# A fused transformer step on one core: the last part of the down projection moved into the common sequence, and one more gate half computed by seven block products

## The chip, the cores and the metric

The kernel runs on one core of a Trainium2 chip. The engines that matter are TensorE (PE, with its weight loads PEld), VectorE (DVE), ScalarE (ACT), GpSimd (POOL) and SyncE (SP), which issues most of the loads. The metric is the device time of one execution in microseconds, as the median of several runs. The trace and the profile page come from one execution taken by the hardware profiler; its own time and its span are given below.

## The reference

One layer of a hybrid backbone over 640 tokens (128 context, 512 latent): adaptive RMSNorm, two parallel token mixers (retention and attention), a gated merge with residual, then a second adaptive RMSNorm and a gated MLP with a depthwise convolution of width 3, residual, and a final RMSNorm. The change is in the MLP alone:

```python
def conv_ffn(h, w_up, conv_w, conv_b, w_down):
    L = h.shape[1]
    u = h @ w_up                                   # 640 x 1024 times 1024 x 5632
    up = jnp.pad(u, ((0, 0), (1, 1), (0, 0)))
    uc = conv_w[0] * up[:, :L] + conv_w[1] * up[:, 1:L + 1] + conv_w[2] * up[:, 2:L + 2] + conv_b
    a, g = jnp.split(uc, 2, axis=-1)               # value half, gate half: 2816 columns each
    return (jax.nn.silu(g) * a) @ w_down           # 2816 x 1024
...
xs = xs + g2 * conv_ffn(h, w_up[l], conv_w[l], conv_b[l], w_down[l])
...
y_sample = rmsnorm(xs, final_g)
```

All inputs are float32. The kernel splits each operand into a high part of the type fp32r and a remainder, and a product is three matmuls: high x high, high x remainder, remainder x high.

## The kernel before

**Tiling.** The 2816 columns of the MLP are 22 blocks of 128, called `f`; two neighbours form a pair `p` (0 to 10). For each pair there is a value half (`i` = 0) and a gate half (`i` = 1). The normalised input, with columns for the convolution's edges, is `h2`: two tiles (high and remainder) of 8 blocks of rows by 2 x 322 columns. Up products are made in column pieces of 322 (`HW`), one PSUM bank each.

**Two forms of an up half.** `plain_group(p, i)` (line 1259) computes it directly: four pieces (two blocks, two column halves) of 8 x 3 = 24 matmuls, 96 in all, with `up_cols` (line 1119). `unit_group(p, i)` (line 1283) uses a scheme of seven block products (numbered m = 1, 5, 6, 2, 3, 7, 4 in their order): each is 4 x 3 = 12 matmuls of 322 columns, 84 in all, on sums and differences of quarters. The sums of weight blocks are formed for every half by VectorE in the raw weight buffer, and the sums of quarters of `h2` once, in `sa[1]` to `sa[4]`. `sa[4]` is made last, by `last_sum` (line 1203), and overwrites the quarter `aq[1, 0]` of `h2` itself. Product m3 reads `sa[4]`; m2, m3, m6, m7 and m4 add onto results of earlier ones, m6, m7 and m4 in m1's bank. Before, pair 0 and both halves of pair 1 are computed directly, and pairs 2 to 10 by block products.

**After the up products.** ScalarE and VectorE copy the banks into `ub`; `conv(f, i)` (line 1130) makes a row of 641 from it (four such row buffers, tag `row`), and `gate(f)` (line 1139) computes the activation of block `f` and writes it, high part and remainder, into the tiles `gt0` and `gt1`, one pair of tiles per pair of blocks, two buffers each. These functions are put on a list `later`, of which one is issued behind each TensorE item.

**Down products.** `down_groups` (line 1356) multiplies finished blocks with rows of `w_down` (blocks 0 and 1, then four blocks at a time), for 5 row tiles `t` and two halves of 512 output columns, into banks `acc`; partial sums are collected in `x1`. The last four blocks, 18 to 21, are treated apart behind the loop: `last_mm` runs first halves (parts 0 and 1, that is blocks 18 and 19) for four row tiles and both column halves, which fill all eight banks, and then the second halves (blocks 20 and 21); each finished bank is scaled and added by `down_add`, squared, and `finish` normalises and writes out.

**Weights.** `w_raw` loads 1 MB into one of two raw buffers (tag `raw`) through SP's queue. `w_split` (line 138) makes high parts by a ScalarE cast (line 146), and remainders in one of two ways: by VectorE's subtraction (line 151), or, with `"dma"`, by a negated ScalarE pass (line 148) and an accumulating DMA of GpSimd (line 149). The results live in eight tiles (tag `wh`) of 1024 columns. A block product takes one such tile, half of a down group of four blocks takes four.

**The order around the change.** The groups form one list; TensorE's items are issued in that order by hand (`manual_schedule`), except that the seventh product of a `unit_group` (m4) is held back until two items of the next group have gone. The weight preparations are sorted by the place of their first product, and `pump` (line 1404) issues a load when fewer than two loaded groups still have preparations open, and a preparation when it and the live ones fit into eight tiles. The order on ScalarE, VectorE and the queues within these limits is fixed at compile time. The last w_down part was outside: its two halves were loaded and split behind the loop, with VectorE's subtraction, and its first products followed the last m4.

Of the kernel before, what the change touches and what calls it, by code (L numbers as in the profile page):

```python
# [18 lines left out]
P = 128  # L19
DM = 1024  # L20
KD = DM // P
NT = 5
# [4 lines left out]
NF = FF // P  # L27
# [41 lines left out]
def hybrid_step(ctx: ExitStack, tc: tile.TileContext, a: dict, o: dict):  # L69
# [60 lines left out]
    def load_w(src, kk, n, lo_eng=None):  # L130
        return w_split(w_raw(src, kk, n), kk, n, lo_eng)

    def w_raw(src, kk, n):
        raw = wp([P, 4 * 512], F32, tag="raw", bufs=2)
        nc.sync.dma_start(raw[:, :kk * n].rearrange("p (k n) -> p k n", n=n), src.rearrange("(k p) n -> p k n", p=P))
        return raw

    def w_split(raw, kk, n, lo_eng=None):
        hs, ls = [], []
        step = 1024 // n  # L140
        for k0 in range(0, kk, step):
            w = min(step, kk - k0) * n
            rv = raw[:, k0 * n:k0 * n + w]
            hi = wp([P, 1024], F32R, tag="wh", bufs=8)[:, :w]
            lo = wp([P, 1024], F32R, tag="wh", bufs=8)[:, :w]
            nc.scalar.copy(hi, rv)  # L146
            if lo_eng == "dma":
                nc.scalar.activation(lo, rv, AF.Copy, scale=-1.0)
                nc.gpsimd.dma_start(lo, rv, accum_op=ALU.add)
            else:  # L150
                (lo_eng or V).tensor_sub(lo, rv, hi.bitcast(F32))  # L151
            for k in range(w // n):
                hs.append(hi[:, k * n:(k + 1) * n])
                ls.append(lo[:, k * n:(k + 1) * n])
        return hs, ls

    def mm3(ps, ah, al, bh, bl, start, stop):
        nc.tensor.matmul(ps, ah, bh, start=start, stop=False)  # L158
        nc.tensor.matmul(ps, ah, bl, start=False, stop=False)  # L159
        nc.tensor.matmul(ps, al, bh, start=False, stop=stop)  # L160
# [127 lines left out]
    mm = Pool("mm1", 5, space=PSUM)  # L288
# [233 lines left out]
    for i in (1, 0):  # L522
        ct, st = ctab[i], stab[i]
# [72 lines left out]
    mm = Pool("mm2", 1, space=PSUM)  # L596
# [129 lines left out]
    mm = Pool("mm3", 5, space=PSUM)  # L726
# [118 lines left out]
    st = states()  # L845
# [168 lines left out]
    def gt_pair():  # L1014
        return [gtp([P, 2, 2 * HW], F32R, tag=f"gt{i}", bufs=2) for i in range(2)]
# [7 lines left out]
    def x_row(dtype=F32):  # L1023
        return x1p([P, 768], dtype, tag="row", bufs=4)
# [3 lines left out]
    w_out, w_up, w_down = a["w_out"][0], a["w_up"][0], a["w_down"][0]  # L1028
# [40 lines left out]
    raw = w_raw(w_up[:, :256], 8, 256)  # L1069
# [6 lines left out]
    with tc.manual_schedule(engines={ET.PE}):  # L1076
        bank = {}
# [52 lines left out]
    def conv(f, i):  # L1130
        u, q = ub[f % 2][i], i * NF + f
        v = cvs[f, i] = x_row()[:, :641]
        nc.scalar.activation(v, u[:, 1:642], AF.Identity, scale=cw[:, 1, q:q + 1], bias=cw[:, 3, q:q + 1])
        V.scalar_tensor_tensor(v, u[:, 0:641], cw[:, 0, q:q + 1], v, op0=ALU.mult, op1=ALU.add)
        V.scalar_tensor_tensor(v, u[:, 2:643], cw[:, 2, q:q + 1], v, op0=ALU.mult, op1=ALU.add)
# [3 lines left out]
    def gate(f):  # L1139
        if f // 2 not in gts:  # L1140
            gts[f // 2] = gt_pair()
        r = [x[:, f % 2, :641] for x in gts[f // 2]]
        ca, cg = cvs[f, 0], cvs[f, 1]
        tg = t7([P, 641], tag="tg", bufs=1)
        nc.scalar.activation(tg, cg, AF.Tanh, scale=0.5)
        V.scalar_tensor_tensor(cg, tg, 1.0, cg, op0=ALU.add, op1=ALU.mult)
        V.tensor_mul(ca, ca, cg)
        nc.scalar.copy(r[0], ca)
        V.tensor_sub(r[1], ca, r[0].bitcast(F32))
# [17 lines left out]
    acc = Pool("acc7", 4, space=PSUM)  # L1167
    mm = Pool("mm7", 4, space=PSUM)
# [88 lines left out]
    later = []  # L1257

    def plain_group(p, i):
        st = {}  # L1260

        def load():
            st["raw"] = w_raw(w_up[:, i * FF + 2 * p * P:i * FF + 2 * (p + 1) * P], 8, 256)

        def prep():
            st["w"] = w_split(st["raw"], 8, 256, "dma")

        def bank(f, h):
            def go():
                up_cols(f, i, st["w"], h * HW, (h + 1) * HW)  # L1270
                if h:
                    if i and f % 2:
                        last_sum()
                    later.append(lambda: conv(f, i))
                    if i and f % 2:
                        later.append(lambda: gate(f - 1))
                        later.append(lambda: gate(f))
            return go

        items = [bank(2 * p + f, h) for f in range(2) for h in range(2)]  # L1280
        return load, [(prep, 4, items)], items
# [74 lines left out]
    def down_groups(fs, step, after=()):  # L1356
        rows = slice(fs[0] * P, (fs[-1] + 1) * P)

        def group(g):
            st = {}  # L1360

            def load():
                st["raw"] = w_raw(w_down[rows, g * 512:(g + 1) * 512], len(fs), 512)

            def prep():
                st["w"] = w_split(st["raw"], len(fs), 512, "dma")

# [12 lines left out]

    d0 = down_groups([0, 1], 0)
    groups = [plain_group(1, 0), d0[0], plain_group(1, 1), d0[1]]
    for p in range(2, NF // 2):
        groups += [unit_group(p, 0), unit_group(p, 1)]
        if p % 2:
            d = down_groups(list(range(2 * p - 4, 2 * p)), 2 if p == 9 else 1, (2 * p + 1, 2 * p))
            groups = groups[:-1] + [d[0], groups[-1], d[1]]
    seq, held = [], []
    for _, _, items in groups:
        for x in items[:-1] if len(items) == 7 else items:  # L1390
# [34 lines left out]
    for fn in later:  # L1425
        fn()

    fs = list(range(NF - 4, NF))
    rows = slice(fs[0] * P, NF * P)
    ws = [load_w(w_down[rows, g * 512:(g + 1) * 512], 4, 512) for g in range(2)]  # L1430
    fg = wp([P, 4 * 512], F32, tag="raw", bufs=2)[:, :DM]
    nc.sync.dma_start(fg, a["final_g"].unsqueeze(0).to_broadcast([P, DM]))
    cols = {t: ((0, 512), (512, 256), (768, 256)) if t == NT - 1 else ((0, 512), (512, 512)) for t in range(NT)}
    bank = {}

    def last_mm(t, c0, n, part):
        if (t, c0) not in bank:
            pool, tag = ((acc, "acc"), (mm, "mm"))[t % 2]
            bank[t, c0] = pool([P, 512], tag=tag)[:, :n]
        g, cc = c0 // 512, slice(c0 % 512, c0 % 512 + n)  # L1440
        down_mm(bank[t, c0], t, fs, [[x[:, cc] for x in y] for y in ws[g]], part)

    with tc.manual_schedule(engines={ET.DVE, ET.PE}):
        for t in range(NT - 1):
            for c0, n in cols[t]:
                last_mm(t, c0, n, (0, 1))
        for t in range(NT):
            for c0, n in cols[t]:
                last_mm(t, c0, n, (2, 3) if t < NT - 1 else (0, 1, 2, 3))
                down_add(bank[t, c0], t, c0)  # L1450
                square(t, c0, n)
                if c0 == 0 and t == 3:
                    finish(0, 3)
        finish(NT - 2, 2)
# [37 lines left out]
```

## Time and profile before

| | us |
|---|---|
| median of 3 runs | 1202.6 (1199.58 to 1203.64) |
| profiled execution, its time | 1202.29 |
| its span, first to last instruction | 1200.5 |
| TensorE busy | 1160.6 |
| VectorE busy | 736.5 |
| ScalarE busy | 567.1 |
| mean granted TensorE clock | 0.992 |
| gate half of pair 1, on TensorE | 790.86 to 805.16 |
| last block product and first halves of the last down products | 1151.40 to 1168.27 |
| second halves, to the last matmul | 1168.27 to 1185.3 |

How to read it: times inside the span count from its start. A busy share is a mean over stages with different limits. A row of an instruction gives its start, its length, engine and line, what it writes and reads, and in brackets the idle time of its engine before it and what ended it. Tiles have a name and a running number, such as `weights.wh.396`.

### The profile page before, as it was taken

The page shows a single profiled execution, that of the slowest core. Times are in us where ns is not written, and L with a number is a line of the kernel's source. Part 1 is how long each engine was busy: PE and PEld are TensorE (multiplying, and loading weights), DVE is VectorE, ACT ScalarE, POOL GpSimd, SP SyncE. Part 2 cuts the span into 40 slices and gives each one's busy share as a digit, 9 for nine tenths or more (in the row PEclk, how much of TensorE's full clock was granted, in tenths as well). Part 3 has the DMA queues.
Part 4 walks back from the last instruction along what each step waited for, and adds up shares of the span by engine and source line. Part 5 has one row for each costly group of instructions (what it writes and reads, how often), then busy time and mean ns, then how long its engine had stood idle before and what let it go on. Part 6 is the DMA issues. An engine that isn't in the chain of part 4 may idle for free.

```text
span 1200.5 us, 18330 instructions
## 1 busy us (share of the span) xinstructions
PE 1160.6 (97%) x7329; PEld 1043.8 (87%) x7329; DVE 736.5 (61%) x1428; ACT 567.1 (47%) x1013; POOL 173.9 (14%) x181
## 2 busy tenths in 40 slices
PE   4999999999999999999999999999999999999994
PEld 3788899999988888889999988999899898998884
DVE  5676977763234436453323259947677597677877
ACT  4345756551132324433322236667557465574453
POOL 0032200000012100042111122011111121122102
PEclk9999999999999999999999999999999999999998
DMA  8832111115564431112122459346657556677532
GB/s 283 273 113 71 36 36 36 36 59 166 198 215 148 141 97 44 36 36 70 39 92 82 158 126 184 89 113 116 139 140 170 131 105 133 128 136 171 120 96 87
DMA packets 129509, 139.54 MB, mean 116 GB/s; under 512 B 26240, under 2 KB 96976, under 8 KB 129424
## 3 DMA queue, kind: packets, MB, share of 16 engines
q1 hardware_dynamic: 104432, 109.01, 28.1%
q0 software_dynamic: 24272, 28.05, 14.4%
q8 instruction: 57, 0.93, 0.3%
q10 hardware_dynamic: 720, 1.31, 0.3%
q14 instruction: 28, 0.23, 0.1%
HBM read 110.31 MB, written 6.03 MB: 97 GB/s over the span
## 4 chain that ended last, share of the span: by engine, by line
PE 82%; DVE 8%; ACT 3%; issue 2%; DMA 2%; POOL 1%; SPq 0%; DVEq 0%; ACTq 0%; POOLq 0%
DMA weights.wh.379_10430<-weights.raw.369_10202 1%; DVE acts.u2.2_101 L1065 1%; DVE x1.u1.1_6381 L1224 1%; DMA xin.u1.1_112<-in_x_sample 0%; DMA weights.wh.394_10721<-weights.raw.382_10453 0%; DMA weights.raw.402_10915<-in_w_down 0%; POOL f0.s.5_3525 L901 0%; DVE acts.u1.1_100 L1064 0%; DVE x1.u1.1_6381 L1037 0%; DVE x1.u1.1_6381 L1254 0%; DVE gt.gt0.5_7260 L1175 0%; PE mm1.mm.11_318 L158 0%; PE mm7.mm.46_9644 L1327 0%; PE mm7.mm.34_8912 L1327 0%; PE mm7.mm.22_8180 L1327 0%
## 5 line engine op out<-in xcount | busy, mean ns | idle before, releaser
L790 POOL TENSOR_TENSOR ret.r2k.6_3635<-ret.u5.5_3528,ret.u1.1_3521 128x256 f32<-128x256 f32 x2 | 1.4, 740 | 205.0 <-ACT ret.u5.5_3528 L786 205.0
L1251 POOL TENSOR_TENSOR x1.u1.1_6381<-x1.u1.1_6381,weights.raw.407_10925 128x512 f32<-128x512 f32 x5 | 7.5, 1502 | 39.6 <-ACT x1.tm.112_10994 L1241 28.3
L839 DVE SCALAR_TENSOR_TENSOR ret2.u1.1_4322<-ret2.u1.1_4322,const.u14.14_94 64x128 f32<-64x128 f32 x24 | 6.8, 336 | 6.6 <-ACT ret2.u1.1_4322 L832 6.5
L1338 DVE TENSOR_TENSOR t7.u4.4_6930<-t7.u4.4_6930,const.u1.1_70 128x322 f32<-128x322 f32 x9 | 4.5, 496 | 10.1 <-ACT const.u1.1_70 L1337 10.1
L524 POOL TENSOR_TENSOR p1.u1.1_618<-p1.u3.3_622,p1q.u1.1_612 128x512 f32<-128x512 f32 x1 | 1.6, 1600 | 59.5 <-DMA p1.u4.4_624<-in_cache_k 59.5
L355 PE MATMUL mm1.mm.1_180<-const.u1.1_70,xin.u1.1_112 128*128 128x128 f32 x4 | 1.1, 434 | 9.3 <-DVE xin.u1.1_112 L348 9.3
L151 DVE TENSOR_TENSOR weights.wh.183_6570<-weights.raw.181_6567,weights.wh.182_6569 128x1024 fp32r<-128x1024 f32 x1 | 1.2, 1226 | 14.3 <-ACT weights.wh.182_6569 L146 14.3
L841 DVE SCALAR_TENSOR_TENSOR ret2.u1.1_4322<-ret2.u1.1_4322,const.u14.14_94 64x128 f32<-64x128 f32 x24 | 6.6, 382 | 4.8 <-ACT ret2.u1.1_4322 L834 4.8
L792 DVE TENSOR_TENSOR ret.u5.5_3528<-ret.u5.5_3528,ret.u1.1_3521 128x512 f32<-128x512 f32 x5 | 3.5, 693 | 9.4 <-POOL ret.r2k.8_3706 L790 3.3
L355 PEld LDWEIGHTS mm1.mm.1_180<-const.u1.1_70,xin.u1.1_112 128*128 128x128 f32 x4 | 0.7, 216 | 9.5 <-DVE xin.u1.1_112 L348 9.5
L392 ACT CAST acts.u1.1_100<-f0.s.1_113 128x640 fp32r<-128x640 f32 x4 | 2.9, 729 | 12.9 <-DVE f0.s.1_113 L390 12.9
L792 DVE TENSOR_TENSOR ret.u4.4_3527<-ret.u4.4_3527,ret.u1.1_3521 128x512 f32<-128x512 f32 x5 | 3.5, 692 | 9.0 <-POOL ret.r2k.11_3886 L790 4.7
L392 ACT CAST acts.u1.1_100<-f0.s.2_114 128x640 fp32r<-128x640 f32 x4 | 2.9, 730 | 9.9 <-DVE f0.s.2_114 L390 9.9
L151 DVE TENSOR_TENSOR weights.wh.108_4352<-weights.raw.106_4349,weights.wh.107_4351 128x1024 fp32r<-128x1024 f32 x1 | 1.2, 1226 | 10.3 <-ACT weights.wh.107_4351 L146 10.3
L901 POOL TENSOR_TENSOR f0.s.5_3525<-f0.s.5_3525,ret2.ny20.11_4904 128x512 f32<-128x512 f32 x5 | 6.0, 1238 | 9.1 <-DVE ret2.ny20.11_4904 L218 9.1
L146 ACT CAST weights.wh.112_4507<-weights.raw.111_4505 128x1024 fp32r<-128x1024 f32 x1 | 1.1, 1050 | 13.3 <-PE mm3.mm.36_4220 L159 13.3
L493 ACT ACTIVATE f0.s.3_724<-f0.s.3_724,p1q.ny20.11_892 128x128 f32<-128x128 f32 x20 | 6.0, 388 | 2.5 <-DVE p1q.ny20.11_892 L216 2.5
L828 POOL DMA_DIRECT2D out_new_state_ret_fwd<-ret.r2k.25_4345 x1 | 0.7, 662 | 43.8 <-ACT ret.r2k.25_4345 L827 43.8
L258 DVE COPY mod2.wr.9_4312<-aux3.aux.15_4279 128x128 f32<-128x128 f32 x1 | 0.3, 291 | 10.9 <-PE aux3.aux.15_4279 L255 10.9
L1235 DVE TENSOR_TENSOR x1.u1.1_6381<-x1.u1.1_6381,gate.u1.1_5311 128x512 f32<-128x512 f32 x10 | 6.7, 687 | 0.0
L1338 DVE TENSOR_TENSOR t7.u3.3_6929<-t7.u3.3_6929,const.u1.1_70 128x322 f32<-128x322 f32 x9 | 4.4, 494 | 3.4 <-ACT const.u1.1_70 L1337 3.4
L146 ACT CAST weights.wh.182_6569<-weights.raw.181_6567 128x1024 fp32r<-128x1024 f32 x1 | 1.1, 1055 | 11.5 <-PE mm3.mm.83_6401 L159 11.5
(7021 smaller groups left out, 4887.1 us busy)
## 6 DMA issues: line engine op xcount, KB each, us to landing
spill.u1.1_6389<-x1.u1.1_6381 POOLq DMA_DIRECT2D x5, 512.0 KB, 4.4
xin.u1.1_112<-in_x_sample SPq DMA_DIRECT2D x4, 512.0 KB
p0.u5.5_130<-in_w_mod SPq DMA_DIRECT2D x2, 1024.0 KB
p0.u6.6_135<-in_w_mod SPq DMA_DIRECT2D x2, 1024.0 KB
p0.u7.7_138<-in_w_mod SPq DMA_DIRECT2D x2, 1024.0 KB
mod.wm.2_2921<-in_w_mod SPq DMA_DIRECT2D x1, 2048.0 KB
mod.wm.4_3072<-in_w_mod SPq DMA_DIRECT2D x1, 2048.0 KB
mod.wm.6_3227<-in_w_mod SPq DMA_DIRECT2D x1, 2048.0 KB
```

The costliest lines, as they stand in the source:

```text
L151: (lo_eng or V).tensor_sub(lo, rv, hi.bitcast(F32))
L392: nc.scalar.copy(hT[0][:, k, :], xk)
L493: nc.scalar.activation(x[:, j], x[:, j], AF.Copy, scale=rstd[:, j:j + 1])
L792: V.tensor_mul(z, z, r1[:, t, 0:1, :].to_broadcast([P, 8, 64]))
L839: V.scalar_tensor_tensor(Ss[0:64, hh, st + 1, j], Ss[0:64, hh, st, j], cdsel[0:64, h:h + 1], Ss[0:64, hh, st + 1, j], op0=ALU.mult, op1=AL ...
L841: V.scalar_tensor_tensor(Ss[64:128, hh, 2 - st, j], Ss[64:128, hh, 3 - st, j], cdsel[64:128, h:h + 1], Ss[64:128, hh, 2 - st, j], op0=ALU. ...
L901: nc.gpsimd.tensor_mul(ov, ov, rso[:, 4 * t:4 * t + 4].unsqueeze(2).to_broadcast([P, 4, P]))
L1065: V.tensor_sub(d[1], hm, d[0].bitcast(F32))
L1224: V.tensor_add(x1[:, t, gs], x1[:, t, gs], tm)
L1235: V.tensor_mul(x1[:, t, gs], x1[:, t, gs], gb[:, t == 0, gs])
L1251: nc.gpsimd.tensor_mul(x1[:, t, lo], x1[:, t, lo], fg[:, lo])
L1338: V.tensor_sub(u[1][:, hi_u], u[1][:, hi_u], u3[i])
```

## The change

```diff
@@ plain_group
                 if h:
-                    if i and f % 2:
+                    later.append(lambda: conv(f, i))
+                    if f % 2:
                         last_sum()
-                    later.append(lambda: conv(f, i))
-                    if i and f % 2:
-                        later.append(lambda: gate(f - 1))
-                        later.append(lambda: gate(f))
@@ list of groups
-    d0 = down_groups([0, 1], 0)
-    groups = [plain_group(1, 0), d0[0], plain_group(1, 1), d0[1]]
+    d0 = down_groups([0, 1], 0, (3, 2))
+    groups = [plain_group(1, 0), d0[0], unit_group(1, 1), d0[1]]
...
+    fs = list(range(NF - 4, NF))
+    cols = {t: ((0, 512), (512, 256), (768, 256)) if t == NT - 1 else ((0, 512), (512, 512)) for t in range(NT)}
+    bank, ws = {}, {}
+
+    def last_mm(t, c0, n, part):
...
+    def last_group(g):
+        st = {}
+
+        def load():
+            st["raw"] = w_raw(w_down[fs[0] * P:, g * 512:(g + 1) * 512], 4, 512)
+
+        def prep():
+            ws[g] = w_split(st["raw"], 4, 512, "dma")
+
+        items = [lambda t=t: last_mm(t, g * 512, 512, (0, 1)) for t in (0, 2, 1, 3)]
+        return load, [(prep, 4, items)], items
+
+    groups += [last_group(0), last_group(1)]
@@ behind the loop
-    fs = list(range(NF - 4, NF))
-    rows = slice(fs[0] * P, NF * P)
-    ws = [load_w(w_down[rows, g * 512:(g + 1) * 512], 4, 512) for g in range(2)]
     fg = wp([P, 4 * 512], F32, tag="raw", bufs=2)[:, :DM]
     nc.sync.dma_start(fg, a["final_g"].unsqueeze(0).to_broadcast([P, DM]))
...
     with tc.manual_schedule(engines={ET.DVE, ET.PE}):
-        for t in range(NT - 1):
-            for c0, n in cols[t]:
-                last_mm(t, c0, n, (0, 1))
         for t in range(NT):
             for c0, n in cols[t]:
                 last_mm(t, c0, n, (2, 3) if t < NT - 1 else (0, 1, 2, 3))
```

It does two things. The gate half of pair 1 becomes a `unit_group`; for this `last_sum` is issued with the last piece of pair 1's value half, and the gates of blocks 3 and 2 follow the second down group of blocks 0 and 1. And the first halves of the last down products become two groups of four items in the common list, ordered t = 0, 2, 1, 3 for the first 512 output columns and then for the second. Their loads and preparations are thereby placed by `pump`, the remainders are made through the accumulating DMA, and the held m4 of pair 10's gate half goes behind two of these items. `last_mm` itself is moved and not changed.

More of the change, by code (lines that the diff above doesn't have):

```diff
@@ L1387, in hybrid_step @@
             groups = groups[:-1] + [d[0], groups[-1], d[1]]
+    fs = list(range(NF - 4, NF))
+    cols = {t: ((0, 512), (512, 256), (768, 256)) if t == NT - 1 else ((0, 512), (512, 512)) for t in range(NT)}
+    bank, ws = {}, {}
+    def last_mm(t, c0, n, part):
+        if (t, c0) not in bank:
+            pool, tag = ((acc, "acc"), (mm, "mm"))[t % 2]
+            bank[t, c0] = pool([P, 512], tag=tag)[:, :n]
+        g, cc = c0 // 512, slice(c0 % 512, c0 % 512 + n)
+        down_mm(bank[t, c0], t, fs, [[x[:, cc] for x in y] for y in ws[g]], part)
+    def last_group(g):
[7 more added lines that the diff above has]
+    groups += [last_group(0), last_group(1)]
     seq, held = [], []
@@ L1426, in hybrid_step @@
         fn()
-    fs = list(range(NF - 4, NF))
-    rows = slice(fs[0] * P, NF * P)
-    ws = [load_w(w_down[rows, g * 512:(g + 1) * 512], 4, 512) for g in range(2)]
     fg = wp([P, 4 * 512], F32, tag="raw", bufs=2)[:, :DM]
     nc.sync.dma_start(fg, a["final_g"].unsqueeze(0).to_broadcast([P, DM]))
[L1433 to L1441, printed above, removed]
     with tc.manual_schedule(engines={ET.DVE, ET.PE}):
-        for t in range(NT - 1):
-            for c0, n in cols[t]:
-                last_mm(t, c0, n, (0, 1))
         for t in range(NT):
```

## The prediction

> **What bounds the kernel now.** I read the page's head first, then the waits of TensorE in the whole span, then a table of windows over the last 63 us, then the order of time on each engine there.
>
> ```profile
> span 1200.5 us, 18330 instructions
> PE 1160.6 (97%) x7329; PEld 1043.8 (87%) x7329; DVE 736.5 (61%) x1428; ACT 567.1 (47%) x1013; POOL 173.9 (14%) x181
> ...
> PE mm7.mm.64_10766 L1324 <- ACT const.u1.1_70 L1337: 2.1, 1, 2.1
> ```
>
> TensorE is busy 97% of the span, and in the gated MLP its waits are small; the largest, 2.1 us, stands before the last block product. So a TensorE instruction that goes there shortens the time by its own length, up to the place where another engine sets the end. The windows (length, then busy us and instructions of PE, PEld, DVE, ACT, POOL, the granted clock, DMA share, GB/s) show that place:
>
> ```profile
> 1137.75:1151.40 13.65, 13.00 (x87) 12.51 (x85) 12.95 (x23) 9.52 (x17) 2.58 (x2) 1.00 0.74 172
> 1151.40:1168.27 16.87, 14.75 (x62) 12.23 (x61) 10.91 (x16) 7.48 (x10) 0.00 (x0) 0.90 0.13 50
> 1168.27:1185.30 17.03, 17.02 (x85) 14.10 (x83) 14.74 (x30) 6.25 (x16) 6.25 (x4) 1.00 0.00 0
> 1185.30:1200.50 15.20, 0.00 (x0) 0.00 (x0) 9.30 (x26) 4.67 (x12) 1.26 (x1) 0.61 0.46 173
> ...
> 1169.86 0.69 DVE L1223 TENSOR_TENSOR x1.tm.111_10991<-acc7.acc.51_10929,gate.u1.1_5311 128x512 f32<-128x512 f32 x1 [2.26 <-PE acc7.acc.51_10929 L160]
> ```
>
> At 1168.27 TensorE begins the second halves (output blocks 20 and 21) of the last down products; the first finished bank starts VectorE at 1169.86, and from there VectorE's chain runs to the end. So the end follows the start of these second halves, S = 1168.27, one to one. The change moves S twice: by the block products near 790 us and by what TensorE does between 1151.40 and S.
>
> **Part A, block products in pair 1's gate half.** Two windows, filtered to one of the three lines of each form:
>
> ```profile
> 790.86:805.16 14.30, 9.97 (x32) 6.02 (x32) 1.00 0.49 152
> 812.14:824.51 12.37, 8.64 (x28) 5.28 (x28) 1.00 0.60 124
> ```
>
> The first is the plain gate half: 3 lines x 32 = 96 matmuls of 322 columns in 14.30 us. The second is a half by seven products (pair 2's): 3 x 28 = 84 in 12.37 us. Gain **1.93 us**; one product is 12.37/7 = 1.77. Added beside it are VectorE's block sums and seven weight preparations. They are hidden by idle time on VectorE just there, 6.45 and 7.32 us:
>
> ```profile
> 787.21 0.89 DVE L1134 SCALAR_TENSOR_TENSOR x1.row.62_7442<-t7.u3.3_6929,t7.u5.5_6935,x1.row.62_7442 128x641 f32<-128x641 f32 x1 [6.45 <-ACT x1.row.62_7442 L1133]
> 796.35 0.69 DVE L1310 TENSOR_TENSOR weights.wh.215_7486<-weights.raw.211_7433,weights.wh.215_7486 128x512 fp32r<-128x512 f32 x1 [7.32 <-ACT weights.wh.215_7486 L1305]
> 803.94 1.27 ACT L1188 CAST acts.u1.1_100<-gt.gt0.5_7260 128x1288 fp32r<-128x1288 f32 x1
> 805.41 1.49 DVE L1191 TENSOR_TENSOR acts.u2.2_101<-gt.gt0.5_7260,acts.u1.1_100 128x1288 fp32r<-128x1288 f32 x1
> ```
>
> The block sum `sa[4]` overwrites a quarter of `h2`, so it may be written once the value half of pair 1 is read, five short down products earlier than the new gate half begins (790.86). Its 1.27 + 1.49 us then have until the fifth product, 790.86 + 4 x 1.77 = 797.9: hidden. Without these covers the whole 1.93 would be lost (a rival). Gates 3 and 2 move behind the second down group; their readers are pair 3's down products, behind all of pair 2's block products: nothing.
>
> **Part B, the last w_down part in the sequence.** Its two halves I call L0 and L1 (512 output columns each). Work of TensorE from 1151.40 to S is unchanged: eight first halves and one held block product (m4 of pair 10's gate half).
>
> ```profile
> 1158.49:1168.27 9.78, 9.78 (x43) 7.88 (x42) 8.17 (x10) 3.66 (x5) 0.00 (x0) 1.00 0.01 2
> 1155.00:1157.00 2.00, 2.00 (x9) 2.00 (x9) 1.07 (x5) 1.19 (x2) 0.00 (x0) 0.50 0.00 0
> 1158.50:1160.00 1.50, 1.50 (x8) 1.25 (x7) 1.50 (x2) 0.77 (x1) 0.00 (x0) 1.00 0.05 11
> 1152.95 1.04 ACT L146 CAST weights.wh.403_10917<-weights.raw.402_10915 128x1024 fp32r<-128x1024 f32 x1 [4.80 <-DMA weights.raw.402_10915<-in_w_down]
> 1153.90 0.42 ACT L1337 COPY const.u1.1_70<-mm7.mm.64_10766 128x322 f32<-128x322 f32 x1
> 1154.03 1.23 DVE L151 TENSOR_TENSOR weights.wh.404_10918<-weights.raw.402_10915,weights.wh.403_10917 128x1024 fp32r<-128x1024 f32 x1 [3.04 <-ACT weights.wh.403_10917 L146]
> ```
>
> Seven first halves take 9.78 us, one 1.40. 8 x 1.40 + 1.77 = 12.97 of 16.87; **3.9 us are lost**: 2.1 in the wait (ScalarE's weight cast stands before the bank's copy and waits for a load), most of the rest because the granted clock stays at 0.50 for some 3 us after it (it is back at 1.00 by 1158.5), and half of 3 us is 1.5. If nothing waits in the new order (L0 x2, m4, L0 x2, L1 x4), S = 1151.40 + 12.97 = 1164.4.
>
> But L1's weights come late. Both loads follow from the two raw buffers, and the low parts now go by a ScalarE pass and an accumulating transfer in place of VectorE's subtraction (1.23 us):
>
> ```profile
> 1080.02 0.37 SPq L135 DMA_DIRECT2D weights.raw.367_10179<-in_w_up  x1
> 1106.78 0.37 SPq L135 DMA_DIRECT2D weights.raw.380_10434<-in_w_up  x1
> 1147.70 0.37 SPq L135 DMA_DIRECT2D weights.raw.402_10915<-in_w_down  x1
> ...
> 1144.99 1.06 ACT L146 CAST weights.wh.398_10907<-weights.raw.397_10905 128x1024 fp32r<-128x1024 f32 x1
> 1076.55 1.07 ACT L148 ACTIVATE weights.wh.366_10175<-weights.raw.358_10031 128x1024 fp32r<-128x1024 f32 x1
> 1086.20 0.62 ACT L1305 CAST weights.wh.370_10226<-weights.raw.367_10179 128x512 fp32r<-128x512 f32 x1 [0.81 <-DMA weights.raw.367_10179<-in_w_up]
> 1115.49 0.62 ACT L1305 CAST weights.wh.383_10469<-weights.raw.380_10434 128x512 fp32r<-128x512 f32 x1 [3.15 <-DMA weights.raw.380_10434<-in_w_up]
> 1079.30 0.69 DVE L1310 TENSOR_TENSOR weights.wh.368_10199<-weights.raw.350_9894,weights.wh.368_10199 128x512 fp32r<-128x512 f32 x1
> ...
> weights.wh.364_10170<-weights.raw.358_10031 POOLq DMA_DIRECT2D x1, 512.0 KB, 4.5
> weights.wh.366_10175<-weights.raw.358_10031 POOLq DMA_DIRECT2D x1, 512.0 KB, 4.9
> weights.wh.379_10430<-weights.raw.369_10202 POOLq DMA_DIRECT2D x1, 512.0 KB, 7.8
> ...
> x1.tm.104_10585<-spill.u1.1_6389 POOLq DMA_DIRECT2D x1, 256.0 KB, 6.1
> ```
>
> Step by step, on before's times (A shifts all of it alike):
> - L0: first cast at 1144.99, as now; its four ScalarE passes of about 1.0 end near 1148.9. The first low part is passed by 1147.0 and lands 4.9 later, 1151.9, against a need at 1151.63: wait 0.3 (0 to 3.2 with the 7.8 row; L1's chain doesn't hang on it).
> - L1's raw buffer is pair 10's gate buffer. It is free when m4's weights are made from it, and the planner now sorts that preparation behind L0's four tiles. The neighbour is the last sequence of this shape: last L0-like pass at 1076.55, m4-like subtraction ended 1079.99, 3.4 us. From a last pass at 1147.9 that is 1151.3; the earliest is 1147.7, today's issue. I take 1150.0, m4's cast (0.6) and subtraction (0.7) directly behind the last pass's end, with their starts overlapping a little as in the rows.
> - The load: 5.2 us alone (1147.70 to the cast at 1152.95), 6.2 beside the end of one accumulate (1080.02 to 1086.20), 8.7 beside two (1106.78 to 1115.49). L0's second accumulate runs beside it to about 1154: I take 6.2, landing 1156.2.
> - Two ScalarE passes: 1158.2. Accumulate 4.5 to 7.8, taken 4.9: **1163.1**.
>
> TensorE wants it at 1151.40 + 0.3 + 4 x 1.40 + 1.77 + 0.23 = 1159.3. It waits 3.8 us, more than the 2.1 that cost the clock, so 1.5 on top: S = 1163.1 + 5.4 (what is left of four first halves) + 1.5 = 1170.0, which is **1.7 later** than today. VectorE loses four subtractions (4 x 1.23 = 4.9 us), ScalarE gains four passes, GpSimd four DMA issues in a window where it does nothing (0.00 above), and SP's load of `final_g` comes once L0's buffer is free, about 1154, while GpSimd, its first reader, works only in the window after S: all off the path. For these the cover is the wait itself; SP's queue holds nothing else behind L1's load.
>
> The gates of blocks 21 and 20 were next in line:
>
> ```profile
> 1157.88 0.43 ACT L1342 COPY t7.u2.2_6928<-mm7.mm.64_10766 128x322 f32<-128x322 f32 x1 [1.25 <-PE mm7.mm.64_10766 L1327]
> 1166.77 0.83 DVE L1149 TENSOR_TENSOR gt.gt1.28_10892<-x1.row.108_10808,gt.gt0.27_10891 128x641 fp32r<-128x641 f32 x1 [0.80 <-ACT gt.gt0.27_10891 L1148]
> ```
>
> From the copy behind m4's end (1157.88) to the last gate's end (1167.60) 9.7 us pass. In the new order m4 ends near 1156.3, the gate is done near 1166.1: covered by L1's wait, and late by 1.4 if that wait is gone.
>
> **Two rules beside rows.** The row first: from 1143.90 to 1147.50 only accumulates move data.
>
> ```profile
> 1143.90:1147.50 3.60, 3.60 (x26) 3.60 (x25) 3.44 (x6) 3.60 (x7) 0.00 (x0) 1.00 1.05 118
> ```
>
> They fill the DMA engines (share 1.05) at 118 GB/s. The Trainium skill, "DMA: Bandwidth & Descriptors", section "Issuing engines are not separate DMA queues", says that transfers of all issuers run on the same 16 engines and interleave, which speaks against loading L1 beside L0's accumulates. By that rule the load would be the 8.7 row and S 2.5 later. On the clock, the wait of 2.1 us above was enough for 0.50. The Trainium skill, "TensorE: Matmul & The Clock Gate", Part 1, puts the drop after an idle window of about 3.4 us; this trace disagrees in length. By the page a wait between 2.1 and 3.4 us would be free of the 1.5.
>
> **Sum.** -1.93 + 1.7 = -0.2 us against the profiled execution (1202.29 us, span 1200.5 and 1.8 around it): **1202.1 us**. The median of the runs, 1202.6, is 0.3 above that execution. About 0.3% (3.6 us) is what a measurement of this kernel can tell from no change.
>
> **Rivals.**
> 1. L1 arrives nearly in time: buffer free at 1147.7, load 5.2, passes 2.0, accumulate 4.5 make 1159.4, no clock loss. The gate is next (1164.4 to 1166.1), S 2.2 to 3.9 earlier, total 4.1 to 5.8 less: about 1197.3. For it: the 4.80 us in which ScalarE idles before 1152.95. Against: m4's place behind L0.
> 2. Slower: L1's load and accumulate crowd with L0's accumulates. Load 8.7 and accumulate 7.8 put L1 at 1168.5, S at 1175.4, total 7.1 - 1.9 = 5.2 more: 1207.5. It decides from an arrival of 1166.8 on. For it: the raw.380 and wh.379 rows; against: those had spill reloads (the 6.1 row) beside them, and here none is left, since only pair 9's down groups reload.
> 3. ScalarE again takes L1's cast before the copy that frees m4's bank: m4 starts behind 1156.2 + 1.04 + 0.42 = 1157.7, 3.2 late plus 1.5, ends 1160.9, its gate 9.7 later sets S = 1170.6, +2.3: 1202.7.
> 4. The block products do not do what they say, since their preparations are late on the eight weight tiles: A is lost, 1202.29 + 1.7 = 1204.0.
>
> **How the numbers follow.** Forecast (L1 between 1161 and 1166.8) 0.52, rival 1 0.22, rival 2 0.15, rival 3 0.06, rival 4 0.05. Forecast, 3 and 4 stay within 0.3%: 0.63. Faster by over 0.3%: 0.22 (rival 1). Slower: 0.15 (rival 2). The range takes in most of rivals 1 and 2: 1197.0 to 1206.8.
>
> **What would show it.** Seven products of 1.77 us in pair 1's gate half and no wait there (A right); L1's load issued near 1148.1 (1150.0 less A), TensorE waiting once for a DMA into an L1 tile, with the granted clock at 0.50 after it (B right). Wrong if that wait is under 1 us, if ScalarE or the gate is named there instead, or if VectorE's chain no longer starts with the first finished bank.

## The result: 0.5% slower, and the profile after

| | before | after |
|---|---|---|
| median of 6 runs each, us | 1201.47 (1199.46 to 1203.64) | 1207.4 (1207.17 to 1207.91) |
| span of the profiled execution, us | 1200.5 | 1205.8 |
| mean granted TensorE clock in it | 0.992 | 0.989 |

The ratio is 1.0051 [1.0038, 1.0064]: the change makes the kernel slower, and the time lies 0.6 us above the predicted range. The head of the page after, then TensorE's waits from 700 us on, then SP's from 1100 us on:

```profile
span 1205.8 us, 18338 instructions
PE 1159.6 (96%) x7317; PEld 1041.4 (86%) x7317; DVE 737.5 (61%) x1439; ACT 571.7 (47%) x1023; POOL 177.8 (15%) x185
```

```profile
PE acc7.acc.53_10967 L159 <- DMA weights.wh.407_10926<-weights.raw.404_10827: 5.3, 1, 5.3
PE acc7.acc.53_10967 L158 <- ACT weights.wh.406_10925 L146: 1.6, 1, 1.6
PE mm7.mm.12_7691 L1321 <- ACT t7.u1.1_6927 L1326: 1.3, 1, 1.3
```

```profile
SPq L135 <- DMA weights.wh.403_10823<-weights.raw.395_10677: 15.9, 1, 15.9
```

The 2.1 us before the last block product is gone. (In before, three matmuls of the last part already ran ahead of that product, from 1151.40 on; not all of its first products followed the last m4.) In its place TensorE waits 1.6 + 5.3 = 6.9 us for L1's first high and low part (`wh.406`, `wh.407`), and there is a new wait of 1.3 us in pair 2. SP's row says what L1's load waited for: the accumulating transfer into `wh.403`, which is L0's second low part.

The windows of after (length, busy us and instructions of PE, PEld, DVE, ACT, POOL, granted clock, DMA share, GB/s). The first two lie around the wait in pair 2; 1151.84 is the start of L0's first product and 1173.63 is S, the start of the second halves:

```profile
812.10:815.33 3.23, 1.93 (x15) 1.67 (x13) 3.16 (x5) 3.21 (x7) 0.00 (x0) 1.00 0.86 98
815.33:847.33 32.00, 32.00 (x217) 32.00 (x217) 27.75 (x50) 24.80 (x43) 6.79 (x6) 1.00 0.70 140
...
1151.84:1173.63 21.79, 14.87 (x62) 11.79 (x61) 9.38 (x15) 9.33 (x12) 1.69 (x2) 0.84 0.55 139
1173.63:1190.66 17.03, 17.03 (x85) 14.07 (x83) 14.71 (x30) 6.25 (x16) 6.23 (x4) 1.00 0.00 0
1190.66:1205.80 15.14, 0.00 (x1) 0.00 (x0) 9.30 (x26) 4.67 (x12) 1.26 (x1) 0.60 0.46 173
1163.04:1169.87 6.83, 3.06 (x7) 2.48 (x8) 3.22 (x4) 2.75 (x4) 0.85 (x2) 0.50 0.83 156
```

The last two stages are as long as before (17.03 + 15.14 against 17.03 + 15.20). The stretch from the first of the last products to S has grown from 16.87 to 21.79 us, **4.92 more**, and its clock is 0.50 from 1163.04 to 1169.87, the first 3.8 us of which fall into the wait. L0's first product starts 0.44 later than before (1151.84 against 1151.40) though pair 1's gate half is shorter. Together that is 5.36, and the spans differ by 5.3.

**Where L1 comes from.** The order of time on SP, ScalarE, VectorE and GpSimd:

```profile
1149.06 0.85 POOL L149 DMA_DIRECT2D weights.wh.403_10823<-weights.raw.395_10677  x1 [1.02 <-ACT weights.wh.403_10823 L148]
1151.62 0.69 DVE L1307 TENSOR_TENSOR weights.wh.405_10847<-weights.raw.385_10464,weights.wh.405_10847 128x512 fp32r<-128x512 f32 x1
1154.62 0.37 SPq L135 DMA_DIRECT2D weights.raw.404_10827<-in_w_down  x1
1159.91 1.04 ACT L146 CAST weights.wh.406_10925<-weights.raw.404_10827 128x1024 fp32r<-128x1024 f32 x1 [1.88 <-DMA weights.raw.404_10827<-in_w_down]
1162.21 0.84 POOL L149 DMA_DIRECT2D weights.wh.407_10926<-weights.raw.404_10827  x1 [12.29 <-ACT weights.wh.407_10926 L148]
```

and the DMA issues between 1130 and 1175 us, with the time from issue to landing at the end:

```profile
weights.wh.401_10818<-weights.raw.395_10677 POOLq DMA_DIRECT2D x1, 512.0 KB, 4.6
weights.wh.403_10823<-weights.raw.395_10677 POOLq DMA_DIRECT2D x1, 512.0 KB, 5.4
weights.wh.407_10926<-weights.raw.404_10827 POOLq DMA_DIRECT2D x1, 512.0 KB, 4.6
```

L0's second accumulate is issued at 1149.06 and takes 5.4, so it reads L0's raw buffer (`raw.395`) until about 1154.5; L1's load is issued at 1154.62. It needs 5.3 us to the cast, two ScalarE passes and GpSimd's issue bring the transfer of L1's first low part to 1162.21, and 4.6 later, at 1166.8, TensorE goes on. No time here is over 0.5 us longer than the prediction's rows of 5.2 for the load and 4.9 for the accumulate, so crowding is not what makes L1 late.

**Where the gain of pair 1 goes.** Its products run as forecast, 10.61 us for the first six (790.87 to 801.48), and pair 2's value half begins at 810.33 against 812.14 before. Then, again in order of time:

```profile
794.19 0.69 DVE L1307 TENSOR_TENSOR weights.wh.216_7516<-weights.raw.203_7306,weights.wh.216_7516 128x512 fp32r<-128x512 f32 x1 [4.51 <-ACT weights.wh.216_7516 L1302]
794.91 0.37 SPq L135 DMA_DIRECT2D weights.raw.215_7499<-in_w_up  x1
802.18 0.62 ACT L1302 CAST weights.wh.218_7535<-weights.raw.215_7499 128x512 fp32r<-128x512 f32 x1 [5.38 <-DMA weights.raw.215_7499<-in_w_up]
814.86 0.41 ACT L1326 COPY t7.u1.1_6927<-mm7.mm.12_7691 128x322 f32<-128x322 f32 x1
```

The load for pair 2's value half is issued when the last of pair 1's seven preparations (m4, `wh.216`) has read its raw buffer, at 794.91. ScalarE stands idle for 5.38 us with that load's first cast at the head of its order, and the copy that frees the bank of pair 2's first product comes at 814.86. The bank is wanted for the third product, so TensorE waits 1.3 us, and at the next long products (847.33 against 847.55) 0.22 us is left of 1.81.

### The profile page after: what moved, and what is told of

It reads as the page before. It is cut to its first block, busy times and chain, and to the rows that moved or that the text cites. A ratio compares the mean times of both kernels' runs of the same rounds, so it can differ in the third digit from the quotient of the medians.

```text
span 1205.8 us, 18338 instructions
## 1 busy us (share of the span) xinstructions
PE 1159.6 (96%) x7317; PEld 1041.4 (86%) x7317; DVE 737.5 (61%) x1439; ACT 571.7 (47%) x1023; POOL 177.8 (15%) x185
## 4 chain that ended last, share of the span: by engine, by line
PE 78%; DVE 8%; DMA 4%; issue 4%; ACT 3%; POOL 1%; SPq 0%; DVEq 0%; POOLq 0%; ACTq 0%
DMA t7.u5.5_6935<-in_conv_w 1%; DMA weights.raw.383_10445<-in_w_up 1%; DVE x1.u1.1_6381 L1224 1%; POOL x1.u1.1_6381 L1037 1%; DMA xin.u1.1_112<-in_x_sample 0%; DMA weights.wh.403_10823<-weights.raw.395_10677 0%; DMA weights.raw.395_10677<-in_w_down 0%; DMA weights.raw.404_10827<-in_w_down 0%; POOL f0.s.5_3525 L901 0%; DVE acts.u2.2_101 L1065 0%; DMA weights.wh.407_10926<-weights.raw.404_10827 0%; DMA x1.u1.1_6381<-in_x_prompt 0%; DVE x1.u1.1_6381 L1236 0%; DVE acts.u1.1_100 L1064 0%; DVE x1.u1.1_6381 L1254 0%
```

## The experiments

The table gives for each kernel the ratio to before with its interval, the start of pair 2's first long down product (`acc.11`) and of L0's first product (`acc.51`), both counted from the first short down product (`acc.1`, 783.88 us in before), and the stretch from there to S. The starts are read from the order of time on TensorE. They are counted from this mark because it lies itself between 780.73 and 784.15 us, and the mean granted clock of the first 60 us differs with it: 1.00 in the three earliest (`a_only`, `v_rem0`, `half_u`), 0.94 in the three latest (after, `v_rem`, `v_rem1`). None of the changes touches that stretch, and a median of few runs can move with it. Beside each kernel before ran again; its medians there are 1201.72 (runs from `a_only` to `v_rem`), 1201.86 (from `v_rem1` to `v_rem_u`) and 1202.0 (`m4_first`), and the ratios are against these. From S to the end of the span it is 32.2 to 32.7 us in every kernel but `half_l1` (34.5).

| kernel | median, us | ratio | long products | L0 | L0 to S |
|---|---|---|---|---|---|
| before | 1201.47 | | 63.67 | 367.52 | 16.87 |
| after | 1207.4 | 1.0051 [1.0038, 1.0064] | 63.44 | 367.95 | 21.79 |
| a_only | 1199.85 | 0.9989 [0.9976, 1.0001] | 63.50 | 367.44 | 14.88 |
| b_only | 1208.27 | 1.0063 [1.0040, 1.0086] | 63.67 | 367.78 | 22.74 |
| half_l1 | 1204.29 | 1.0023 [1.0008, 1.0037] | 63.46 | 367.29 | 17.03 |
| v_rem | 1198.54 | 0.9976 [0.9964, 0.9988] | 63.44 | 367.58 | 13.09 |
| v_rem1 | 1202.18 | 1.0002 [0.9993, 1.0012] | 63.46 | 367.82 | 17.15 |
| v_rem0 | 1200.56 | 0.9992 [0.9984, 1.0001] | 63.44 | 367.23 | 16.92 |
| half_u | 1204.99 | 1.0033 [1.0020, 1.0045] | 61.86 | 365.98 | 22.03 |
| v_rem_u | 1195.87 | 0.9951 [0.9938, 0.9964] | 61.86 | 365.98 | 12.95 |
| m4_first | 1204.29 | 1.0020 [1.0008, 1.0032] | 63.52 | 367.39 | 19.83 |

**One part alone.** `a_only` is the kernel before with the block products of pair 1 and nothing else:

```diff
-    d0 = down_groups([0, 1], 0)
-    groups = [plain_group(1, 0), d0[0], plain_group(1, 1), d0[1]]
+    d0 = down_groups([0, 1], 0, (3, 2))
+    groups = [plain_group(1, 0), d0[0], unit_group(1, 1), d0[1]]
...
```

> Only the gate half of pair 1 by seven block products; the last down part as before. Theory: the 1.93 us gained on TensorE are given back almost whole by a wait of 1.3 us in the third product of pair 2's value half, because ScalarE is behind there; at the first long down product (847.55 before) TensorE is 0.2 to 0.3 us early, and the end moves by 0 to -0.4 us against before. Rival, the gain holds and the last part costs all: 1.9 us less than before.

`b_only` is the changed kernel with this undone. 

> Only the last down part moved into the sequence; pair 1 as before. Theory: the stretch from the last block product before it to the second halves grows from 16.9 to about 21.8 us, and the time is 4.5 to 5.5 us above before. Rival, the gain of pair 1 holds in the whole change and this part costs more: 7 us above before.

In `b_only` the stretch to S is 22.74 us and the waits for L1 are those of after, 1.5 and 5.3: the last part's move makes the loss by itself. It is larger than the 4.5 to 5.5 us expected: the median is 6.6 above before's, and the stretch 0.95 longer than in after, since the clock stays at half for longer (shown at the end). In `a_only` the lead is as small as in after: 0.17 us at the long products and 0.08 at the last part. Its span is 5.3 us shorter than before's for other reasons: 3.15 us lie ahead of `acc.1`, and 2.0 in the tail that this kernel has in common with before. TensorE's wait there, and the windows around and behind it:

```profile
PE mm7.mm.63_10777 L1321 <- ACT const.u1.1_70 L1334: 1.7, 1, 1.7
```

```profile
1148.17:1150.69 2.52, 0.86 (x6) 0.38 (x4) 0.35 (x1) 1.43 (x3) 0.00 (x0) 1.00 0.80 273
1150.69:1153.69 3.00, 3.00 (x17) 2.82 (x18) 2.07 (x5) 2.53 (x4) 0.00 (x0) 1.00 0.00 0
```

The same wait is 1.7 us in place of 2.1, and the clock behind it stays at 1.00, where before has 0.50. That is the 2.0 us by which its stretch is shorter. Its runs reach from 1197.01 to 1201.69 us, and the interval takes in 1, so this is no gain that can be credited to the block products. The median is 1.9 us under before's, the rival's number, but the lead that the rival needs is not there.

**L1's first blocks in a buffer of their own.** `half_l1` loads blocks 18 and 19 of L1 into 4 KB per partition beside the two raw buffers; line numbers above 137 are 4 or 5 higher in it.

```diff
-            st["raw"] = w_raw(w_down[fs[0] * P:, g * 512:(g + 1) * 512], 4, 512)
+            src = w_down[fs[0] * P:, g * 512:(g + 1) * 512]
+            if g:
+                st["raw"] = [w_load(rz([P, 1024], tag="h"), src[:2 * P], 2, 512), w_raw(src[2 * P:], 2, 512)]
+            else:
+                st["raw"] = w_raw(src, 4, 512)
...
```

> The whole change, but the rows of blocks 18 and 19 of L1 are loaded into 4 KB per partition of their own, so this load waits for no raw buffer; remainders still by the accumulating transfer. Theory (L1's load waits for L0's second accumulate, whose buffer it takes): the load is issued before 1145, the remainder lands before its product, the two waits of TensorE for L1 (1.6 and 5.3 us) go, the gates are next, the second halves start at 1165 to 1167 instead of 1173.6, and the time falls by 6.5 to 8.5 us, to 1199 to 1201. Rival (accumulates and loads crowd each other on the DMA engines): a wait of 3 us or more for the accumulate into L1 stays, and the time falls by under 3 us.

It falls by about 3 us against after and not by what was expected. TensorE's largest wait, ScalarE's rows behind it, and the window from L0 to S:

```profile
PE acc7.acc.51_10902 L162 <- ACT gt.gt0.27_10951 L1153: 3.9, 1, 3.9
```

```profile
1157.65 1.05 ACT L150 CAST weights.wh.408_10935<-weights.raw.404_10832 128x1024 fp32r<-128x1024 f32 x1 [5.19 <-DMA weights.raw.404_10832<-in_w_down]
1158.60 0.42 ACT L1344 COPY t7.u2.2_6931<-mm7.mm.63_10778 128x322 f32<-128x322 f32 x1
```

```profile
1150.20:1167.23 17.03, 13.12 (x63) 10.62 (x61) 8.31 (x15) 7.60 (x11) 1.69 (x2) 1.00 0.63 147
```

The wait for L1 is gone: 13.12 us of work, all of it done at a clock of 1.00. But the other half of L1 still goes through L0's buffer, its cast stands ahead of the copy of m4's bank on ScalarE, ScalarE idles 5.19 us for it, and the gate is late. This is the mechanism of rival 3, for another half of the weights: a wait moved, not removed. What the stretch gains against after, 4.8 us, is half lost again behind S, where the wait's price falls due:

```profile
1167.30:1170.60 3.30, 3.30 (x8) 2.45 (x9) 1.14 (x2) 0.00 (x0) 0.00 (x0) 0.50 0.00 0
```

TensorE works at half clock there, and S to the end is 2.3 us longer than in after, 1.7 of it on TensorE.

**The remainders on VectorE.** `v_rem` takes the subtraction again for both halves:

```diff
-            ws[g] = w_split(st["raw"], 4, 512, "dma")
+            ws[g] = w_split(st["raw"], 4, 512)
```

> The whole change, but the remainders of L0 and L1 by VectorE's subtraction instead of the accumulating transfer. Theory: L0's buffer is free about 5 us earlier, at the end of its second subtraction, L1's load is issued near 1149.5, its remainder is ready 3.5 us after the landing, near 1158, and TensorE waits at most 1 us for L1; the time is 1199.5 to 1202. Rival (the load itself or the place in the sequence costs): the wait stays above 3 us and the time stays above 1204.

```profile
1148.38 1.22 DVE L151 TENSOR_TENSOR weights.wh.403_10822<-weights.raw.395_10677,weights.wh.402_10821 128x1024 fp32r<-128x1024 f32 x1
1149.63 0.37 SPq L135 DMA_DIRECT2D weights.raw.404_10825<-in_w_down  x1
1150.32 0.69 DVE L1307 TENSOR_TENSOR weights.wh.405_10845<-weights.raw.385_10464,weights.wh.405_10845 128x512 fp32r<-128x512 f32 x1
```

```profile
1151.73:1164.82 13.09, 13.09 (x63) 10.63 (x61) 10.42 (x17) 7.34 (x10) 0.00 (x0) 1.00 0.30 110
```

It is faster than before, more so than expected. In order of time, L1's load follows the end of L0's second subtraction (1149.60) and starts while pair 10's gate buffer, `raw.385`, is still to be read by m4's subtraction (1150.32). So **the buffer that L1 takes is L0's**. TensorE does not wait at all in the stretch to S: 13.09 us busy in 13.09.

**Which of the two effects it is.** The accumulating transfers of L0 hold the buffer; those of L1 make its own way longer. `v_rem1` uses VectorE for L1 alone, `v_rem0` for L0 alone:

```diff
-            ws[g] = w_split(st["raw"], 4, 512, "dma")
+            ws[g] = w_split(st["raw"], 4, 512, "dma" if g == 0 else None)
```

> The changed kernel, but only L1's remainder by VectorE's subtraction; L0's keeps the two ScalarE passes and the two accumulating transfers. Theory (two terms: the raw buffer that L0's second accumulate frees late, and the remainder's way of about 6 us behind L1's arrival): L1's load is still issued near 1154.6 and lands near 1159.9, cast to 1161, subtraction to 1162.2, need near 1159.2: TensorE waits some 3 us for VectorE (L151), the clock loss stays, and the second halves start near 1169.1 in place of 1173.6: about 4.5 less, 1203. Rival (only the remainder's way counts; the buffer is of no matter): as fast as with both remainders on VectorE, 1198.5.

> The changed kernel, but only L0's remainder by VectorE's subtraction; L1's keeps the ScalarE passes and the accumulating transfers. Theory (two terms): L1's load is issued near 1149.6, as with both remainders on VectorE, lands near 1155, its low pass ends near 1157.5, the accumulate takes 4.6 or somewhat less beside nothing: low part ready near 1162, need near 1159.2, a wait of 2.5 to 3 us for a DMA and the clock loss; second halves near 1169, about 4.5 less than the changed kernel: 1203. Rival (only the buffer counts): no wait of more than 0.5 us, 1198.5 to 1199.5.

TensorE's waits for L1 in `v_rem1`, then in `v_rem0`:

```profile
PE acc7.acc.53_10965 L158 <- ACT weights.wh.406_10925 L146: 1.3, 1, 1.3
...
PE acc7.acc.53_10965 L159 <- DVE weights.wh.407_10926 L151: 0.8, 1, 0.8
```

```profile
PE acc7.acc.53_10965 L159 <- DMA weights.wh.407_10924<-weights.raw.404_10825: 2.1, 1, 2.1
```

L1's load goes out 2.76 us after L0's first product in `v_rem1`, as in after, and 2.15 before it in `v_rem0`. Both effects count. Against after, the stretch to S is 4.6 us shorter with the buffer held and the way short (17.15), and 4.9 shorter with the buffer free and the way long (16.92); with both it is 8.7 shorter (13.09). S in `v_rem1` is 1169.12, as expected to 0.1 us, though TensorE waits 2.1 us in two parts and not some 3 us for VectorE. Both medians came out below the 1203 expected, `v_rem0` by 2.4 us; of that its wait is 0.4 to 0.9 shorter than expected, and L0 starts 0.7 earlier from the mark than in after.

**Pair 2's load.** `half_u` is the changed kernel with the first half of the rows for pair 2's value half loaded into a 4 KB buffer of its own (its line numbers are up to 11 higher):

```diff
-            w = w_raw(w_up[:, i * FF + f0_ * P:i * FF + (f0_ + 2) * P], 8, 256).rearrange("p (k n) -> p k n", n=256)
+            src = w_up[:, i * FF + f0_ * P:i * FF + (f0_ + 2) * P]
+            if (p, i) == (2, 0):
+                w = [w_load(rz([P, 1024], tag="h"), src[:4 * P], 4, 256), w_raw(src[4 * P:], 4, 256)[:, :1024]]
...
```

> The changed kernel, with the first half of the rows of the unit weights of pair 2's value half loaded into a 4 KB buffer of its own, so that this load needn't wait for the subtraction that ends pair 1's seven preparations. Theory (part A's gain is given back because ScalarE sits idle in order before that load's cast and then runs late with the bank copies): the 1.3 us wait in pair 2's third block product goes to under 0.3, the lead at pair 2's short down products is 1.4 to 1.8 us in place of 0.2 to -0.4, and the time is 1.4 to 1.8 less: about 1205.8. Rival (the lead is lost further on in any case, since the planner's due times keep ScalarE and VectorE where they were): the wait goes, another comes within pairs 2 to 4, and the time stays at 1207.4.

ScalarE's first cast for pair 2 in `half_u`, and the window from pair 2's first product to the long down products, first of after and then of `half_u`:

```profile
792.06 0.61 ACT L1313 CAST weights.wh.218_7540<-half.h.1_7502 128x512 fp32r<-128x512 f32 x1
```

```profile
810.33:847.33 37.00, 35.70 (x242) 35.43 (x240) 32.12 (x56) 29.78 (x52) 7.73 (x7) 1.00 0.73 135
```

```profile
807.46:842.88 35.42, 35.42 (x241) 35.41 (x240) 29.97 (x52) 27.00 (x48) 6.76 (x6) 1.00 0.63 126
```

ScalarE no longer idles before this cast, TensorE is busy throughout, and the lead is 1.81 us at the long products and still 1.54 at L0 (365.98 against 367.52). This settles what took the gain of pair 1. The median is 2.4 us under after's where 1.4 to 1.8 were expected; 2.0 of it is L0's earlier start from the mark (365.98 against 367.95).

**Both corrections.** `v_rem_u` has the remainders of `v_rem` and the buffer of `half_u`.

> Both remainders of the last part by VectorE, and the 4 KB buffer for the unit weights of pair 2's value half. If the two corrections add, as their places some 300 us apart suggest: 1198.5 less 1.4 to 1.8, about 1197. Rival (the lead from pair 1 is lost before the end): 1198.5, as with the remainders alone.

```profile
1148.52:1161.47 12.95, 12.95 (x62) 10.67 (x61) 10.41 (x17) 7.33 (x10) 0.00 (x0) 1.00 0.31 112
```

They add: L0 starts 1.54 us earlier from the mark than before, and S follows 12.95 us after it, 3.92 sooner. The end behind S is 0.4 longer (32.63), so 5.1 of the 6.0 us between the medians beside each other (1195.87 and 1201.86) are placed. About 1197 was expected. This version beats both kernels, by 0.49% [0.36%, 0.62%] before's.

**The buffer of the prediction.** `m4_first` keeps the accumulating transfers and sorts m4's preparation ahead of L0's, so that L1 takes the buffer on which the prediction counted:

```diff
-    preps.sort(key=lambda z: z[4])
+    l0 = len(groups) - 2
+    first = pos[id(groups[l0][2][0])]
+    preps.sort(key=lambda z: z[4] - 3 * (z[0] == l0 - 1 and z[4] > first))
```

> The changed kernel, remainders still by accumulating transfers; only the preparation of pair 10's held product m4 is sorted ahead of L0's preparation, so that pair 10's gate buffer, and not L0's, is the one that L1's load takes. Theory (the prediction's step that failed is the buffer that L1's load takes, and not the way behind it): the load is issued near 1146 in place of 1154.6 and is no longer released by L0's second accumulate; L1's first low part is ready by 1161.5; L0's own preparation stands about 1 us later, so TensorE waits 1 to 2 us for it near 1152, and less than 1 us for L1; the second halves start between 1165 and 1168 in place of 1173.6, the time is 1199 to 1202. Rival (GpSimd's accumulating transfers are late whatever buffer is used): TensorE still waits over 3 us for a DMA into an L1 tile, 1204 or more.

SP's wait and L1's load, TensorE's wait, the two transfers of L0, and the window from L0 to S:

```profile
SPq L135 <- DMA weights.wh.397_10716<-weights.raw.385_10464: 7.2, 1, 7.2
```

```profile
1146.77 0.37 SPq L135 DMA_DIRECT2D weights.raw.401_10775<-in_w_down  x1
...
1152.47 1.04 ACT L146 CAST weights.wh.406_10925<-weights.raw.401_10775 128x1024 fp32r<-128x1024 f32 x1 [3.17 <-DMA weights.raw.401_10775<-in_w_down]
```

```profile
PE acc7.acc.51_10897 L159 <- DMA weights.wh.403_10841<-weights.raw.395_10677: 3.8, 1, 3.8
```

```profile
weights.wh.403_10841<-weights.raw.395_10677 POOLq DMA_DIRECT2D x1, 512.0 KB, 7.1
weights.wh.405_10846<-weights.raw.395_10677 POOLq DMA_DIRECT2D x1, 512.0 KB, 7.7
```

```profile
1150.64:1170.47 19.83, 15.98 (x63) 12.96 (x61) 8.30 (x13) 9.11 (x12) 1.69 (x2) 0.83 0.66 144
```

The load goes out at 1146.77 from the gate buffer, and TensorE does not wait for L1 at all. But the load now runs beside L0's accumulates, which take 7.1 and 7.7 us in place of 4.6 and 5.4, and TensorE waits 3.8 us for L0. S comes 19.83 us after L0's first product. Of the 6.7 us over `v_rem`'s 13.09, 3.8 are this wait and 2.9 the half clock behind it (15.98 us busy in place of 13.09). So the theory was right about the buffer and L1, and wrong about L0 and the time: 1199 to 1202 us was missed, and 1204.29 lies in the rival's range, without the wait for L1 that the rival needed. Neither place of m4's preparation makes the accumulating form as good as before. The predicted case itself, this buffer with a load only 1.4 us ahead of L0's first product, was not run; here it is 3.9 us ahead.

## Why the prediction was wrong

**The step that failed** is "L1's raw buffer is pair 10's gate buffer", with a load issued at 1150.0. The planner issues a load when fewer than two loaded groups have preparations open. L0 has one preparation and pair 10's gate half still has m4's, so L0's is the one that closes first, and L1 takes L0's buffer. What ends that buffer's use is then the second accumulate of L0, a transfer that the prediction had running beside the load. From the start of L0's products, the load is issued 2.78 us after it, not 1.4 before it. `v_rem` and `m4_first` show the buffer, `v_rem0` what freeing it is worth.

This step makes 3.2 of the 5.5 us by which the span missed the forecast: 21.79 from L0 to S, where 18.6 was predicted. The other 2.4 are part A, a second step that failed: 1.93 early was forecast for L0, and it came 0.44 late. With either one put right, 1207.4 would have been 1204.2 or 1205.0, inside the range.

- **The way behind the load was right** to within 0.9 us (12.2 where 13.1 was taken). With the measured issue, 1154.62 + 5.3 (load, taken 6.2) + 2.3 (passes and issue) + 4.6 (accumulate, taken 4.9) is 1166.8; adding the predicted 5.4 and 1.5 gives 1173.7, and S is 1173.63.
- **The wait and the clock** came as forecast in kind: a DMA into an L1 tile, and 0.50 behind it. The wait was longer, 6.9 us and not 3.8, and the first 1.6 of it were for the high part's cast. The sign that was to show B right, a load near 1148.1, did not appear.
- **L0** came in time; the 0.3 us wait for its first low part is not there.
- **S to the end, one to one**: 32.17 us after, 32.23 before, and at most 0.5 us longer in other kernels with S from 1161.47 to 1174.26, but for `half_l1` with its half clock behind S.
- **Part A, 1.93 us.** The products were right and so were VectorE's covers. The term "hidden" was wrong one step on: seven preparations hold a raw buffer longer than one does, the next half's load moved from 789.10 to 794.91, and ScalarE, in its fixed order, carried the delay to a bank. The prediction counted preparations against idle time on VectorE and didn't follow the load that they release. Of 1.81 us of lead, 0.22 is left at the long products; at L0 the seven profiled kernels with pair 1's block products and without `half_u`'s buffer lie from 0.29 early to 0.43 late. Two waits on record give that range to within 0.2 us: `acc.46`'s for the DMA into `wh.382` near 1112 us (0.65 to 1.15, 0.83 in before), and that of a block product of pair 10 (`mm.64`) for VectorE near 1140 us (0 to 0.38, none in before). Why these differ was not tried.
- **Rival 1** took its time from a late gate, 1.4 us behind a TensorE that doesn't wait. In `v_rem_u` the stretch to S is 12.95 us, the 12.97 that the prediction worked out for no loss. The gate term is there, but smaller:

```profile
1161.40 0.83 DVE L1154 TENSOR_TENSOR gt.gt1.28_10948<-x1.row.108_10832,gt.gt0.27_10947 128x641 fp32r<-128x641 f32 x1 [0.80 <-ACT gt.gt0.27_10947 L1153]
1162.28 0.51 PE L164 MATMUL acc7.acc.51_10900<-weights.wh.402_10826,gt.gt1.28_10948 128*128 128x512 f32 x1
```

  The last gate ends at 1162.23, 0.8 us behind S (1161.47), and the third matmul of the second halves, the first to read `gt1`, starts right then. The second halves take 17.48 us, 0.45 more than the 17.03 of before and after; so much is the term worth, not 1.4.
- **Rival 2** gave 1207.5, which is the number, but not by its mechanism: the load took 5.3 us and the accumulates 4.6 and 5.4. Crowding appeared only in `m4_first`. **Rival 3** appeared, of the kernels with the new order, only in `half_l1`, and **rival 4**, preparations late on the weight tiles, in no kernel: A was lost behind its products, not in them.

## What to carry to other kernels

When a load is moved into a planned sequence, work out from the planner's rule which buffer it will get and name the last reader of that buffer; an accumulating transfer reads it until it lands (here up to 5.4 us from its issue), a subtraction only until the engine is done (1.2 us). When a stage gets more preparations, follow the buffer that they hold to the next load and that load's first cast, since an engine that works in a fixed order hands a late load on to every copy behind it. A lead is worth something only if it is still there at the next stage, so measure it there.

## What was not expected of the hardware

**Unequal crowding.** A load of 1 MB beside two accumulating transfers of 512 KB (`m4_first`) took 5.7 us to its cast, against 5.3 alone; the transfers took 7.1 and 7.7, against 4.6 and 5.4 (the second of them, issued at 1149.60, also met L1's own first accumulate, issued at 1154.76). The Trainium skill, "DMA: Bandwidth & Descriptors", section "Issuing engines are not separate DMA queues", says that transfers of all issuers interleave on the same 16 engines; the trace agrees, and shows that the accumulating side paid nearly all of it: 2.5 us for the first accumulate, 0.4 for the load.

**The clock after short waits.** One and the same wait left 0.50 behind it at 2.1 us (before) and 1.00 at 1.7 us (`a_only`). In `v_rem0`, `v_rem1` and `b_only` (windows):

```profile
1156.02:1158.70 2.68, 0.56 (x2) 0.49 (x3) 2.42 (x4) 0.85 (x2) 0.55 (x1) 1.00 0.99 185
1158.70:1162.20 3.50, 3.50 (x10) 2.70 (x9) 3.04 (x4) 1.71 (x3) 0.00 (x0) 0.51 0.49 91
```

```profile
1163.00:1163.40 0.40, 0.40 (x4) 0.31 (x3) 0.40 (x1) 0.40 (x1) 0.00 (x0) 1.00 0.16 41
1163.40:1163.70 0.30, 0.30 (x2) 0.28 (x1) 0.30 (x1) 0.23 (x1) 0.00 (x0) 0.50 0.00 0
```

```profile
1161.40:1171.60 10.20, 5.12 (x12) 4.06 (x13) 3.22 (x4) 4.07 (x6) 1.69 (x2) 0.50 0.55 103
```

In the first the clock is at half for 3.4 us after a wait of 2.1; in the second it falls while TensorE is already at work again, behind two waits of 1.3 and 0.8. Added up from windows of 0.1 us, the half clock lasts 3.41 us in before, `half_l1`, `v_rem0` and `v_rem1`, 6.83 in after, `half_u` and `m4_first`, and 10.24 in `b_only`: once, twice and three times 3.41. The Trainium skill, "TensorE: Matmul & The Clock Gate", Part 1, describes a free-running window of about 3.4 us. The lengths agree with it, and so does a fall that isn't tied to the wait's start; that a wait of 2.1 us is enough, well under one window, does not agree with a whole idle window as the condition. In the 3.41 us ahead of the fall TensorE was still busy for 1.3 us in before and 1.8 in `v_rem1`.

So the price of such a wait is not fixed by its length. After and `b_only` wait 6.9 and 6.8 us in the same place, but do 3.06 and 5.12 us of work at half clock, a loss of 1.5 and 2.6 us. How little work in a window makes the clock fall, no run here fixes.
